# Reordering GpSimd and vector work around two RMS statistics of a Trainium2 step

## The chip, the cores and the metric

The kernel runs on one NeuronCore of a Trainium2 chip. Five engines run side by side, each through its own queue in order: TensorE (PE, with its weight loads PEld), VectorE (DVE), ScalarE (ACT), GpSimd (POOL) and SyncE (SP), which here only issues DMAs. They wait for one another through semaphores. The metric is the device time of one execution in microseconds (us), median over several runs.

## The reference

Two trunk layers over 512 latent tokens and 128 context tokens (640 columns in the kernel) with 1024 features, all in float32. Layer 0 is neighbourhood attention, layer 1 a gated linear recurrence; each is followed by a SwiGLU feed-forward. Every sub-layer is normalised first and added back through a gate, and the result is normalised once more. What matters here is the end of layer 1:

```python
def _rms_norm(x, g):
    return x * lax.rsqrt(jnp.mean(x * x, axis=-1, keepdims=True) + RMS_EPS) * g

def _modulate(x, g, shift, scale):
    return _rms_norm(x, g) * (1 + scale[:, None, :]) + shift[:, None, :]

def _swiglu(x, w_gu, w_down):
    gate, up = jnp.split(x @ w_gu, 2, axis=-1)
    return (jax.nn.silu(gate) * up) @ w_down
...
    o, h = _lru_mixer(...)                       # ends in y @ w_out
    x = x + g1 * o
    x = x + g2 * _swiglu(_modulate(x, norm_g, sh2, sc2), w_gu, w_down)
return _rms_norm(x, final_g)
```

## The kernel before

Features lie on partitions (8 tiles of 128, index k or f), tokens along the free axis. Every float32 matrix product is done as three passes in a reduced format: each operand is split into `hi` (ACT casts it) and `lo` (DVE subtracts `hi` from the original), and PE adds hi·hi, hi·lo and lo·hi in PSUM. So each weight tile costs a DMA into a `raw` buffer (three of them in rotation), an ACT cast into `whi` or `whx` and a DVE subtraction into `wlo` or `wlx`. A raw buffer can be loaded again only when its readers are done.

The order on each engine is set by the program's scheduler: it runs over the code with its own time estimates, and the order in which it issues becomes the queue's order. `self.tc.issue_after(ins)` keeps what is written under it from being issued before `ins`; it sets an order and is no wait by itself.

**The output projection of layer 1** (`project_halves`) works on two halves of 320 tokens, CH[0] and CH[1]. For each output tile f a product (`chunk`) lands in PSUM (tiles `mm`, `mx`), DVE adds it to `x` (`residual`, L424), ACT squares the sum (`sq`, two buffers) and DVE adds the squares up in `ssq` (L373, `square`). The instruction of the last such addition is `self.sq`; the last square goes to PE directly.

**The statistic** (`stat`) then runs across the engines: PE multiplies `ssq` and the last square with a column of ones (`at`, L382 and L385), DVE scales it (`var`, L387), GpSimd raises it to the power -1/2 (`rs`, L389), DVE spreads the result on a diagonal (`dg`, L391), and PE multiplies ones with it, so that each partition has the factors of all tokens (`rr`, L394, in a tile named `mx`). In the projection ACT copies that to SBUF (`r`, L744).

**The second feed-forward** (`ffn_halves`) begins with three plain units (PLAIN = 3): gate and up weights, six weight tiles from `unit`, whose splits stand at L177 and L178. `plain(us, 0)` multiplies them with the first half of the tokens, which was normalised earlier, while the statistic of the second half runs. The first weight tile's product may go ahead of `at`; `held` places the first matmul of the second tile behind `at` and its sixth input tile (k = 5) and all later tiles behind `rr`. Then the second half is normalised (L692, L693), split (`xt` and `big`, L1025, L1026), and `plain(us, 1)` uses it. The other hidden units are done by a Strassen-like scheme over halves: it needs sums of input quarters (`sums`: L712 to L714 on DVE and the last on GpSimd, L715, into x) and of weight quarters (`sum_weights`: four subtractions or additions of 128x512 on GpSimd, tile `sum`, L764, that read the raw gate and up weights of a unit).

**The tail** (`project_last`) does the last part of the down projection in two token chunks, CHL = 384 and 256 tokens. After each chunk comes `stat`; the last tile's product (f = 7) of the second chunk is issued behind `rr` of the first. At the end DVE scales the 16 tiles of x with the factors and the final gain (L467) and SP writes `y`.

Of the kernel before, what the change touches and what calls it, by code (L numbers as in the profile page):

```python
# [9 lines left out]
F32 = mybir.dt.float32  # L10
F32R = mybir.dt.float32r
AF = mybir.ActivationFunctionType
ALU = mybir.AluOpType
AX = mybir.AxisListType

P = 128
# [12 lines left out]
NF = FF // P  # L29
# [14 lines left out]
PLAIN = 3  # L44
# [81 lines left out]
class _Step:  # L126
# [33 lines left out]
        return self.t([P, KT, NTOK + 2], dt, "big", 4)[:, :, 0:n]  # L160


    def unit(self, src, slot=None):
        nc = self.nc
        _, a, b = src.shape
        raw = self.t([P, a, b], F32, "raw", 3)
        nc.sync.dma_start(raw, src)
        if slot is None:
            self.nu += 1
            slot = "x" if self.wx and self.nu % 2 == 0 else "m"  # L170
        if slot == "x":
            hi = self.t([P, a, b], F32R, "whx", 3, self.sb)
            lo = self.t([P, a, b], F32R, "wlx", 3, self.sb)
        else:
            hi = self.t([P, a, b], F32R, "whi", 3)
            lo = self.t([P, a, b], F32R, "wlo", 3)
        nc.scalar.copy(hi, raw)  # L177
        nc.vector.tensor_tensor(lo, raw, hi.bitcast(F32), ALU.subtract)  # L178
        return hi, lo

    def two(self, src, x):
# [192 lines left out]
        self.lastq[t0] = q  # L374

    def stat(self, t0, t1):
        nc = self.nc
        bl = [min(b, t1 - P) for b in range(t0, t1, P)]
        n = len(bl)
        ps = self.ps()  # L380
        for j, b in enumerate(bl):
            nc.tensor.matmul(ps[:, j:j + 1], self.ssq[:, b:b + P], self.ones[:, 0:1], start=True, stop=not self.lastq)  # L382
            if not self.lastq:
                continue
            self.at = nc.tensor.matmul(ps[:, j:j + 1], self.lastq[t0][:, b - t0:b - t0 + P], self.ones[:, 0:1], start=False, stop=True).ins  # L385
        v = self.t([P, 8], F32, "var", 2)[:, 0:n]
        self.var = nc.vector.tensor_scalar(v, ps[:, 0:n], 1.0 / D, EPS, ALU.mult, ALU.add).ins  # L387
        r = self.t([P, 8], F32, "rs", 2)[:, 0:n]
        nc.gpsimd.tensor_tensor(r, v, self.mhalf.broadcast_to([P, n]), ALU.pow)  # L389
        dg = self.t([P, 4, P], F32, "dg", 1, self.sb)[:, 0:n]  # L390
        self.dg = nc.vector.tensor_tensor(dg, self.ident.unsqueeze(1).broadcast_to([P, n, P]), r.unsqueeze(2).broadcast_to([P, n, P]), ALU.mult).ins  # L391
        ps = self.ps("rr" if "rr" in self.ptags else "mx")
        for j, b in enumerate(bl):
            self.rr = nc.tensor.matmul(ps[:, b - t0:b - t0 + P], self.ones, dg[:, j], start=True, stop=True).ins  # L394
        self.r = ps, t0
# [55 lines left out]
    def project_last(self, w, hi, lo, gk):  # L451
        G = self.need(self.gcols, gk)
        us, rs, dst = [], [], self.o["y"].rearrange("(k p) t -> p k t", p=P)
        for f in range(0, KT, 2):
            us += self.two(w[f:f + 2], f % 4)
        for c, (t0, t1) in enumerate(CHL):
            for f, u in enumerate(us):
                with self.tc.issue_after(self.rr) if c and f == KT - 1 else nullcontext():
                    ps = self.chunk(u, hi, lo, t0, t1)
                self.residual(f, t0, t1, ps, G, True)  # L460
            self.stat(t0, t1)
            rs.append(self.r[0])
        for (t0, t1), r in zip(CHL, rs):
            for k in range(KT):
                xs = self.x[:, k, t0:t1]
                with self.tc.issue_after(self.sq if k < 3 else self.var if k < 4 else self.dg) if t0 == 0 else nullcontext():
                    self.nc.vector.scalar_tensor_tensor(xs, xs, self.col("fg", k), r[:, 0:t1 - t0], ALU.mult, ALU.mult)  # L467
                if k % 2:
                    self.nc.sync.dma_start(dst[:, k - 1:k + 1, t0:t1], self.x[:, k - 1:k + 1, t0:t1])
# [238 lines left out]
    def sums(self, k, xd):  # L708
        nc = self.nc
        b11, b12, b21, b22 = [self.x[:, j, a:a + HT] for j in (k, k + KH) for a in (0, HT)]  # L710
        t2 = self.t([P, HT], F32, "c22", 2, self.sb)
        nc.vector.tensor_tensor(b11, b12, b11, ALU.subtract)  # L712
        nc.vector.tensor_tensor(t2, b22, b11, ALU.subtract)
        nc.vector.tensor_tensor(b12, b22, b12, ALU.subtract)  # L714
        nc.gpsimd.tensor_tensor(b21, b21, t2, ALU.subtract)  # L715
        for n, v in (("T1", b11), ("T2", t2), ("T3", b12)):
            self.halve(n, k, v)
        nc.sync.dma_start(self.x[:, k], xd[k * P:k * P + P])
# [37 lines left out]
    def sum_weights(self, q):  # L756
        nc, W, g = self.nc, q["W"], q["g"]
        q["u"], src = self.t([P, KT, P], F32, "raw", 3), q["u"]
        nc.sync.dma_start(q["u"], src)
        ss = [self.t([P, KT, P], F32, "sum", 2, self.sb) for _ in range(2)]  # L760
        s1, s2, s3, s4 = [s[:, a:a + KH] for s in ss for a in (0, KH)]
        g1, g2, u1, u2 = [t[:, a:a + KH] for t in (g, q["u"]) for a in (0, KH)]
        for o, x, y, op in ((s1, u1, u2, ALU.add), (s2, s1, g1, ALU.subtract), (s3, g1, u1, ALU.subtract), (s4, g2, s2, ALU.subtract)):
            nc.gpsimd.tensor_tensor(o, x, y, op)  # L764
        for s, names in zip(ss, (("S1", "S2"), ("S3", "S4"))):
            hi, lo = [self.t([P, KT, P], F32R, n, 3, self.sb) for n in ("whx", "wlx")]
            self.split(hi, lo, s)
            for n, a in zip(names, (0, KH)):
                W[n] = hi[:, a:a + KH], lo[:, a:a + KH]
# [83 lines left out]
                self.sums(j, xd)  # L853

    def ffn_halves(self, l, key, xd):
        us = [[self.unit(self.i["gu"][l, c * NF + f]) for c in range(2)] for f in range(PLAIN)]
        self.hold = True
        self.plain(us, 0)
        self.hold = False
# [12 lines left out]
        for ci, n in enumerate(CHN):  # L872
            for j in range(n):
                f = f0 + j
# [302 lines left out]
```

## Time and profile before

| | |
|---|---|
| median of 3 runs | 1556.68 us (1553.93 to 1560.59) |
| profiled execution | 1557.26 us, span from first to last instruction 1555.5 us |
| busy in the span: PE, PEld, DVE, ACT, POOL | 1490.3, 1444.0, 1067.1, 714.9, 205.8 us |
| mean granted TensorE clock | 0.983 of full speed |
| stretch 1050 to 1100 us | PE busy 48.58 us, DVE 30.20, ACT 22.98, POOL 2.31, clock 0.99 |
| stretch 1100 to 1150 us | PE busy 46.38 us, DVE 34.35, ACT 25.05, POOL 10.74, clock 0.90 |
| stretch 1500 to 1556 us | PE busy 42.80 us, DVE 30.48, ACT 12.42, POOL 1.55, clock 0.86 |

Times in the trace count from the span's start. A row of the timeline reads: start, length, engine, line, operation, output<-input, shapes, number of instructions; in brackets how long the engine was idle before it and whose result ended that. A matmul of 128x320 is shown with 0.31 us, but they overlap: the next one starts about 0.15 us later at full clock. The projection's second half and its statistic lie between about 1080 and 1107 us, the tail from about 1517 us to the end.

### The profile page before, as it was taken

How to read it: one execution, taken by the hardware profiler on the slowest of the kernel's cores; microseconds unless marked ns; L12 is line 12 of the kernel's file. 1: busy time of each engine (PE TensorE's matmuls, PEld its weight loads, DVE VectorE, ACT ScalarE, POOL GpSimd, SP SyncE). 2: the span in 40 equal slices, each digit the busy share in tenths (PEclk: the TensorE clock that was granted, in tenths of full speed). 3: DMA queues.
4: the chain of work that ended last, by engine and by line, in shares of the span. 5: the costliest groups of instructions: out<-in, count | busy, mean ns of one | idle time of the engine just before them, and what ended most of it. 6: DMA issues, size and time to landing. Idle time of an engine off the chain costs nothing. (4 is left out here: it accounts for less than half of the span.)

```text
span 1555.5 us, 26069 instructions
## 1 busy us (share of the span) xinstructions
PE 1490.3 (96%) x10315; PEld 1444.0 (93%) x10315; DVE 1067.1 (69%) x2034; ACT 714.9 (46%) x1321; POOL 205.8 (13%) x231
## 2 busy tenths in 40 slices
PE   5999999989999999999999999969899999999996
PEld 4899899879999999999999888869899999999996
DVE  5678788959999887434446489875755656565646
ACT  4576666655332123212334499763544342424232
POOL 2211122100111110000000000000212323232310
PEclk8999999999999999999999999989899999999997
DMA  9535655535666663222223212124232231313111
GB/s 376 159 114 164 170 168 172 155 116 185 190 190 190 201 197 124 72 83 76 68 84 105 70 62 68 55 96 153 89 124 69 82 109 56 108 55 109 55 55 68
DMA packets 69754, 188.25 MB, mean 121 GB/s; under 512 B 7793, under 2 KB 23297, under 8 KB 69505
## 3 DMA queue, kind: packets, MB, share of 16 engines
q1 hardware_dynamic: 57824, 144.49, 29.5%
q0 software_dynamic: 11520, 41.95, 8.8%
q8 instruction: 81, 1.33, 0.4%
q14 instruction: 41, 0.33, 0.1%
q10 hardware_dynamic: 288, 0.16, 0.0%
HBM read 171.09 MB, written 8.92 MB: 116 GB/s over the span
## 5 line engine op out<-in xcount | busy, mean ns | idle before, releaser
L209 PE MATMUL mm<-big,whi 128*128 128x320 f32 (+2 forms) x1290 | 401.8, 315 | 15.9 <-ACT big L1025 8.9
L210 PE MATMUL mm<-big,whi 128*128 128x320 f32 (+2 forms) x1290 | 404.2, 314 | 1.7 <-DVE big L1026 1.3
L211 PE MATMUL mm<-big,wlo 128*128 128x320 f32 (+2 forms) x1290 | 402.8, 313 | 1.0 <-DVE wlo L178 1.0
L209 PEld LDWEIGHTS mm<-big,whi 128*128 128x128 f32 x1290 | 244.7, 191 | 20.4 <-ACT big L1025 9.8
L210 PEld LDWEIGHTS mm<-big,whi 128*128 128x128 f32 x1290 | 245.6, 190 | 5.1 <-DVE big L1026 3.5
L211 PEld LDWEIGHTS mm<-big,wlo 128*128 128x128 f32 x1290 | 245.1, 190 | 2.5 <-DVE wlo L178 1.4
L239 DVE SCALAR_TENSOR_TENSOR mprod<-mraw,csb 128x1024 f32<-128x1024 f32 x160 | 195.4, 1221 | 14.3 <-DMA mraw<-in_wm 13.6
L177 ACT CAST whi<-raw 128x1024 fp32r<-128x1024 f32 (+1 forms) x90 | 93.3, 1037 | 113.5 <-PE mm L210 80.4
L424 DVE SCALAR_TENSOR_TENSOR x<-mm,G,x 128x128 f32<-128x128 f32 (+3 forms) x211 | 85.2, 434 | 86.7 <-PE mm L211 85.8
L178 DVE TENSOR_TENSOR wlo<-raw,whi 128x1024 fp32r<-128x1024 f32 (+1 forms) x90 | 109.6, 1218 | 29.5 <-ACT whi L177 26.6
L211 PE MATMUL mm<-big,wlx 128*128 128x320 f32 (+3 forms) x363 | 112.6, 310 | 0.0
L210 PE MATMUL mm<-big,whx 128*128 128x320 f32 (+3 forms) x363 | 112.4, 310 | 0.0
L209 PE MATMUL mm<-big,whx 128*128 128x320 f32 (+3 forms) x363 | 112.3, 309 | 0.0
L235 POOL DMA_DIRECT2D mraw<-in_wm x80 | 43.4, 542 | 387.1 <-DVE mprod L239 274.7
L209 PE MATMUL mx<-big,whi 128*128 128x320 f32 (+2 forms) x278 | 86.9, 312 | 0.9 <-DVE big L639 0.9
L210 PE MATMUL mx<-big,whi 128*128 128x320 f32 (+2 forms) x278 | 86.4, 311 | 0.0
L211 PE MATMUL mx<-big,wlo 128*128 128x320 f32 (+2 forms) x278 | 86.3, 311 | 0.0
L389 POOL TENSOR_TENSOR rs<-var,mhalf 128x3 f32<-128x3 f32 (+3 forms) x10 | 9.2, 927 | 556.4 <-DVE var L387 556.4
L177 ACT CAST whx<-raw 128x1024 fp32r<-128x1024 f32 (+1 forms) x40 | 41.0, 1028 | 88.8 <-PE mm L210 53.9
L211 PE MATMUL mx<-big,wlx 128*128 128x320 f32 (+3 forms) x245 | 76.3, 312 | 0.7 <-DVE wlx L178 0.7
L209 PE MATMUL mx<-big,whx 128*128 128x320 f32 (+3 forms) x245 | 76.1, 311 | 0.0
L210 PE MATMUL mx<-big,whx 128*128 128x320 f32 (+3 forms) x245 | 76.0, 310 | 0.0
(291 smaller groups left out, 3609.3 us busy)
## 6 DMA issues: line engine op xcount, KB each, us to landing
raw<-in_gu SPq DMA_DIRECT2D x88, 512.0 KB, 3.5
mraw<-in_wm POOLq DMA_DIRECT2D x80, 512.0 KB, 3.9
raw<-in_dn SPq DMA_DIRECT2D x24, 512.0 KB, 3.6
raw<-in_wqk SPq DMA_DIRECT2D x16, 512.0 KB, 4.8
raw<-in_wi SPq DMA_DIRECT2D x16, 512.0 KB, 3.5
raw<-in_dn SPq DMA_DIRECT2D x16, 448.0 KB, 3.3
sw<-in_wm SPq DMA_DIRECT2D x10, 512.0 KB, 10.2
raw<-in_wv SPq DMA_DIRECT2D x8, 512.0 KB, 3.8
```

Of the source, the lines that this page charges most:

```text
L177: nc.scalar.copy(hi, raw)
L178: nc.vector.tensor_tensor(lo, raw, hi.bitcast(F32), ALU.subtract)
L209: nc.tensor.matmul(ps, hi[:, k], xhi[:, k, s], start=(k == 0), stop=False)
L210: nc.tensor.matmul(ps, hi[:, k], xlo[:, k, s], start=False, stop=False)
L211: nc.tensor.matmul(ps, lo[:, k], xhi[:, k, s], start=False, stop=(k == nk - 1))
L235: nc.gpsimd.dma_start(w, self.i["wm"][l * 6 + j - 2, f])
L239: nc.vector.scalar_tensor_tensor(prod, w, 1.0, self.csb[:, s], ALU.mult, ALU.mult, accum_out=out[:, s, f:f + 1])
L389: nc.gpsimd.tensor_tensor(r, v, self.mhalf.broadcast_to([P, n]), ALU.pow)
L424: self.nc.vector.scalar_tensor_tensor(xs, ps[:, a - t0:b - t0], G[:, s, f:f + 1], xs, ALU.mult, ALU.add)
```

## The change

Four edits, in the words of the code:

- `unit` gets an argument `after`: the split's subtraction on DVE is issued behind that instruction. The four weight tiles of the second and third plain unit (`f` = 1, 2) get the last addition of squares in the projection, `self.sq`; the first unit's two tiles get none.
- `stat` is cut into `moment` (`at`, `var`, `rs`, `dg`) and `spread` (`rr`). Elsewhere they still follow each other.
- `sum_weights` issues its four GpSimd instructions behind `self.pw`, which is the latest power (`rs`), and after `sums(0)` and `sums(1)` the GpSimd subtraction of those (`t4`).
- In the tail the first chunk's `spread` is called inside the second chunk's loop ahead of tile f = 5, where before it stood ahead of the whole second chunk; and of the eight scalings of the first chunk, the first three may go after the first chunk's `dg`, the next three after the last addition of squares.

```diff
-    def unit(self, src, slot=None):
+    def unit(self, src, slot=None, after=None):
...
         nc.scalar.copy(hi, raw)
-        nc.vector.tensor_tensor(lo, raw, hi.bitcast(F32), ALU.subtract)
+        with self.tc.issue_after(after) if after else nullcontext():
+            nc.vector.tensor_tensor(lo, raw, hi.bitcast(F32), ALU.subtract)
...
     def stat(self, t0, t1):
+        self.spread(self.moment(t0, t1))
+
+    def moment(self, t0, t1):
...
-        nc.gpsimd.tensor_tensor(r, v, self.mhalf.broadcast_to([P, n]), ALU.pow)
+        self.pw = nc.gpsimd.tensor_tensor(r, v, self.mhalf.broadcast_to([P, n]), ALU.pow).ins
...
+        return t0, bl, dg
+
+    def spread(self, moment):
+        nc = self.nc
+        t0, bl, dg = moment
         ps = self.ps("rr" if "rr" in self.ptags else "mx")
...
+        first = None
         for c, (t0, t1) in enumerate(CHL):
             for f, u in enumerate(us):
+                if c and f == 5:
+                    self.spread(first)
+                    rs.append(self.r[0])
                 with self.tc.issue_after(self.rr) if c and f == KT - 1 else nullcontext():
                     ps = self.chunk(u, hi, lo, t0, t1)
                 self.residual(f, t0, t1, ps, G, True)
-            self.stat(t0, t1)
-            rs.append(self.r[0])
+            if c:
+                self.stat(t0, t1)
+                rs.append(self.r[0])
+            else:
+                first, dg = self.moment(t0, t1), self.dg
...
-                with self.tc.issue_after(self.sq if k < 3 else self.var if k < 4 else self.dg) if t0 == 0 else nullcontext():
+                with self.tc.issue_after(dg if k < 3 else self.sq if k < 6 else self.var if k < 7 else self.dg) if t0 == 0 else nullcontext():
...
-        nc.gpsimd.tensor_tensor(b21, b21, t2, ALU.subtract)
+        t4 = nc.gpsimd.tensor_tensor(b21, b21, t2, ALU.subtract).ins
+        self.pw = t4 if k < 2 else self.pw
...
-            nc.gpsimd.tensor_tensor(o, x, y, op)
+            with self.tc.issue_after(self.pw):
+                nc.gpsimd.tensor_tensor(o, x, y, op)
...
-        us = [[self.unit(self.i["gu"][l, c * NF + f]) for c in range(2)] for f in range(PLAIN)]
+        us = [[self.unit(self.i["gu"][l, c * NF + f], None, self.sq if f else None) for c in range(2)] for f in range(PLAIN)]
```

The instructions are the same in number and shape on every engine; only their order differs, and only in these stretches. Line numbers of the changed program are higher by up to 18. The rows below are the engines' queues; a number behind a name tells one buffer or tile from another of the same name.

GpSimd before, from the projection's first statistic on (`rs_11500` is the power of the second half's statistic, `x` the subtractions of `sums`):

```order
L389 TENSOR_TENSOR rs_11265<-var_11263,mhalf_68 128x3
L764 TENSOR_TENSOR sum_12009<-raw_12007 128x512
L764 TENSOR_TENSOR sum_12010<-raw_11970,raw_12007 128x512
L764 TENSOR_TENSOR sum_12009<-sum_12009,raw_11970 128x512
L389 TENSOR_TENSOR rs_11500<-var_11498,mhalf_68 128x3
L764 TENSOR_TENSOR sum_12010<-raw_11970,sum_12009 128x512
L715 TENSOR_TENSOR x_10897<-x_10897,c_1882_11815 128x320
L715 TENSOR_TENSOR x_10897<-x_10897,c_1886_11882 128x320
```

and after:

```order
L393 TENSOR_TENSOR rs_11265<-var_11263,mhalf_68 128x3
L393 TENSOR_TENSOR rs_11500<-var_11498,mhalf_68 128x3
L731 TENSOR_TENSOR x_10897<-x_10897,c_1882_11815 128x320
L731 TENSOR_TENSOR x_10897<-x_10897,c_1886_11882 128x320
L782 TENSOR_TENSOR sum_12009<-raw_12007 128x512
L782 TENSOR_TENSOR sum_12010<-raw_11970,raw_12007 128x512
L782 TENSOR_TENSOR sum_12009<-sum_12009,raw_11970 128x512
L782 TENSOR_TENSOR sum_12010<-raw_11970,sum_12009 128x512
```

The four sums of the first Strassen unit have gone from around the power to behind the first two subtractions of `sums`.

DVE before, at the end of the projection (`ssq` is the addition of squares, the last of them `sq_11449`; the splits of the plain units' third to sixth weight tile are `wlo_11526`, which stands further up, `wlx_11532`, also further up, `wlo_11538` and `wlx_11544`; `wul` is a split for the first Strassen unit):

```order
L424 SCALAR_TENSOR_TENSOR x_10897<-mx_11461,G_1341_7628,x_10897 128x128
L178 TENSOR_TENSOR wlo_11538<-raw_11535,whi_11537 128x1024
L1026 TENSOR_TENSOR big_10892<-x_10897,big_10892 128x320
L373 TENSOR_TENSOR ssq_10941<-ssq_10941,sq_11371 128x320
L178 TENSOR_TENSOR wlx_11544<-raw_11541,whx_11543 128x1024
L373 TENSOR_TENSOR ssq_10941<-ssq_10941,sq_11410 128x320
L373 TENSOR_TENSOR ssq_10941<-ssq_10941,sq_11449 128x320
L1026 TENSOR_TENSOR wul_12024<-raw_12007,wuh_12023 128x512
L387 TENSOR_SCALAR var_11498<-at_11491 128x3
L391 TENSOR_TENSOR dg_11502<-ident_63,rs_11500 128x384
L692 SCALAR_TENSOR_TENSOR x_10897<-x_10897,A_1176_6453,r_11255 128x192
```

and after:

```order
L1044 TENSOR_TENSOR big_10892<-x_10897,big_10892 128x320
L374 TENSOR_TENSOR ssq_10941<-ssq_10941,sq_11371 128x320
L374 TENSOR_TENSOR ssq_10941<-ssq_10941,sq_11410 128x320
L374 TENSOR_TENSOR ssq_10941<-ssq_10941,sq_11449 128x320
L179 TENSOR_TENSOR wlo_11526<-raw_11523,whi_11525 128x1024
L179 TENSOR_TENSOR wlx_11532<-raw_11529,whx_11531 128x1024
L179 TENSOR_TENSOR wlo_11538<-raw_11535,whi_11537 128x1024
L391 TENSOR_SCALAR var_11498<-at_11491 128x3
L395 TENSOR_TENSOR dg_11502<-ident_63,rs_11500 128x384
L179 TENSOR_TENSOR wlx_11544<-raw_11541,whx_11543 128x1024
L708 SCALAR_TENSOR_TENSOR x_10897<-x_10897,A_1176_6453,r_11255 128x192
```

Four splits of 128x1024 have moved behind the last addition of squares, three of them ahead of `var` and one behind `dg`; `wul` now stands some 20 rows further on, among the second half's work.

PE before, in the tail, between the first chunk's `at` and the second chunk's next product (`mx_15867` is `rr` of the first chunk):

```order
L385 MATMUL at_15854<-ones_72,sq_15852 128x1
L210 MATMUL mm_15977<-big_11510,whx_15716 128x256
L211 MATMUL mm_15977<-big_11509,wlx_15717 128x256
L209 MATMUL mm_15977<-big_11509,whx_15716 128x256
L210 MATMUL mm_15977<-big_11510,whx_15716 128x256
L211 MATMUL mm_15977<-big_11509,wlx_15717 128x256
L394 MATMUL mx_15867<-dg_15865,ones_72 128x128 x3
L209 MATMUL mx_15871<-big_11509,whi_15698 128x256
```

and after, around `rr` (now `mx_15955`):

```order
L210 MATMUL mm_15977<-big_11509,whx_15716 128x256
L211 MATMUL mm_15977<-big_11510,whx_15716 128x256
L212 MATMUL mm_15977<-big_11509,wlx_15717 128x256
L403 MATMUL mx_15955<-dg_15865,ones_72 128x128 x3
L210 MATMUL mx_15959<-big_11509,whi_15710 128x256
L211 MATMUL mx_15959<-big_11510,whi_15710 128x256
L212 MATMUL mx_15959<-big_11509,wlo_15711 128x256
```

Between the last `at` and `rr` PE has 32 matmuls of 128x256 after the change and 5 before; 24 matmuls are left behind `rr`, where 48 were.

## The prediction

> **What bounds the kernel now.** I read the busy shares first, then short windows around the places that the change touches, then the queues of PE, DVE and GpSimd there.
>
> ```profile
> PE 1490.3 (96%) x10315; PEld 1444.0 (93%) x10315; DVE 1067.1 (69%) x2034; ACT 714.9 (46%) x1321; POOL 205.8 (13%) x231
> 1098.00:1107.00 9.00, 5.38 (x27) 5.01 (x27) 3.33 (x3) 0.62 (x1) 6.25 (x5) 0.58 0.20 64
> 1107.00:1128.00 21.00, 21.00 (x136) 21.00 (x136) 19.86 (x51) 13.85 (x40) 5.04 (x3) 0.93 0.12 37
> ```
>
> PE is busy for 96% of the span, so time is to be had only where PE idles or runs slowly. A window's row gives stretch, length, the busy time of PE, PEld, DVE, ACT and POOL, and then the clock: 0.58 of full speed in the nine microseconds around the second half's statistic. Between 1107 and 1128 us PE has no hole; there it has none until the tail either, so what is won ahead of it goes through to the end, unless something that feeds PE is late.
>
> The projection's second statistic, on PE, DVE and POOL:
>
> ```profile
> 1095.08 0.31 PE L845 MATMUL mm<-big,wlo 128*128 128x320 f32 x1
> 1096.71 0.38 PE L382 MATMUL at<-ones,ssq 128*128 128x1 f32 x2 [1.32 <-DVE ssq L373]
> 1105.35 1.62 PE L394 MATMUL mx<-dg,ones 128*128 128x128 f32 x6 [3.62 <-DVE dg L391]
> 1106.62 0.61 PE L843 MATMUL mm<-big,whx 128*128 128x320 f32 x1
> 1109.87 0.31 PE L843 MATMUL mx<-big,whi 128*128 128x320 f32 x1
> ...
> 1091.91 0.67 DVE L424 SCALAR_TENSOR_TENSOR x<-mx,G,x 128x192 f32<-128x192 f32 x2
> 1092.51 1.21 DVE L178 TENSOR_TENSOR wlo<-raw,whi 128x1024 fp32r<-128x1024 f32 x1
> 1093.64 0.48 DVE L1026 TENSOR_TENSOR big<-x,big 128x320 fp32r<-128x320 f32 x1
> 1094.04 0.48 DVE L373 TENSOR_TENSOR ssq<-ssq,sq 128x320 f32<-128x320 f32 x1
> 1098.74 1.64 DVE L1026 TENSOR_TENSOR wul<-raw,wuh 128x512 fp32r<-128x512 f32 x1 [2.08 <-ACT wuh L1025]
> 1100.30 0.15 DVE L387 TENSOR_SCALAR var<-at 128x3 f32<-128x3 f32 x1
> 1103.59 1.62 DVE L391 TENSOR_TENSOR dg<-ident,rs 128x384 f32<-128x384 f32 x1 [3.14 <-POOL rs L389]
> ...
> 1101.49 1.25 POOL L764 TENSOR_TENSOR sum<-sum,raw 128x512 f32<-128x512 f32 x1
> 1102.71 0.85 POOL L389 TENSOR_TENSOR rs<-var,mhalf 128x3 f32<-128x3 f32 x1
> 1103.54 1.25 POOL L764 TENSOR_TENSOR sum<-raw,sum 128x512 f32<-128x512 f32 x1
> ```
>
> PE waits twice, 1.32 us for the additions of squares and 3.62 us for `dg`. The additions end late because splits of about 1.13 us (start 1092.51 to 1093.64) stand between them. `var` (1100.30) waited behind `wul`; the power was ready to start at about 1100.45 and began at 1102.71, behind sums; `dg` took 1.62 us beside the fourth sum. The projection's first statistic shows the same chain with none of this beside it:
>
> ```profile
> 1072.63 0.28 PE L385 MATMUL at<-ones,sq 128*128 128x1 f32 x2
> 1074.47 0.15 DVE L387 TENSOR_SCALAR var<-at 128x3 f32<-128x3 f32 x1
> 1075.65 0.56 DVE L391 TENSOR_TENSOR dg<-ident,rs 128x384 f32<-128x384 f32 x1 [1.03 <-POOL rs L389]
> 1079.21 0.83 PE L394 MATMUL mx<-dg,ones 128*128 128x128 f32 x6
> 1079.80 0.39 PE L209 MATMUL mx<-big,whi 128*128 128x320 f32 x1
> ```
>
> From the start of `var` to the end of `dg` it takes 1.74 us there (1074.47 to 1076.21) and 4.91 us (1100.30 to 1105.21) here; from the start of `at` to that of `var` 1.84 us.
>
> **The change part by part.** *Splits behind the additions.* The last residual (1091.91) comes with PE's product and does not move. Behind it DVE has 0.60 for that residual, 0.40 for the split of `big` and three additions of the same shape, 0.40 each (1093.64 to 1094.04 for one), which ends at 1094.1; with 0.3 for squares that wait for their buffers, 1094.4. So `at` no longer waits: it follows the first plain tile at 1095.24, 1.47 us earlier, and is done by 1097.1 (1.84 us later) at the latest. But three splits now stand ahead of `var`: 1094.4 + 3 x 1.13 = 1097.8, so `var` starts at 1097.9, set by DVE and not by `at`. That is 2.4 us earlier than before.
>
> *Sums behind the power.* The power finds POOL idle and `dg` runs alone: 1.74 us from 1097.9, plus the 0.14 us between `dg` and `rr` (1105.21 to 1105.35), so `rr` starts at 1099.8 instead of 1105.35: 5.55 us. PE still idles there, since the 15 matmuls between `at` and `rr` take 2.2 us at 0.15 each: with some 1.1 us for `at` itself (my estimate, inside those 1.84) they are over at 1098.5, and a gap of 1.3 us is left in place of 3.62.
>
> What is left open is the clock. Before, it had fallen to half, so that `rr` took 1.27 us (1105.35 to 1106.62) where the first statistic's took 0.59. The nearest row of a short gap shortly after an `at` is in the tail (1533.28, below): 1.17 us, and half clock behind it. So I take 5.6 us with no gain from the clock. The other end is full clock throughout: 0.68 us in `rr`, and the twelve matmuls behind it took 3.25 us (1106.62 to 1109.87), where twelve at 0.15 take 1.8; 1.4 more, together 2.1, so 7.7 us. The Trainium skill, "TensorE: Matmul & The Clock Gate", Part 1, says that the clock is halved after an idle window of about 3.4 us, so by it a gap of 1.3 us would leave it full and the middle would gain 7.7 us. The tail's row does not agree with that: half clock after 1.17 us.
>
> *What the moved work could hold up.* The third plain unit's second raw weight tile can be loaded only after the third tile's split:
>
> ```profile
> 1093.74 0.33 SPq L759 DMA_DIRECT2D raw<-in_gu  x1
> 1098.09 0.62 ACT L1025 CAST wuh<-raw 128x512 fp32r<-128x512 f32 x1 [0.95 <-DMA raw<-in_gu]
> 1107.47 0.68 DVE L692 SCALAR_TENSOR_TENSOR x<-x,A,r 128x192 f32<-128x192 f32 x2 [2.26 <-ACT r L744]
> 1121.22 0.48 DVE L1026 TENSOR_TENSOR xt<-x,xt 128x320 fp32r<-128x320 f32 x1
> 1125.86 0.31 PE L844 MATMUL mm<-xt,whi 128*128 128x320 f32 x1
> sw<-in_wm SPq DMA_DIRECT2D x10, 512.0 KB, 10.2
> ```
>
> Such a load took 4.35 us from issue to the cast (1093.74 to 1098.09). The plain tile's is now issued at 1095.6 and lands at 1099.95; its cast on ACT ends at 1101.0, beside `rr`, and ahead of the copy `r` (which ended before 1107.47). Its split ends on DVE at about 1102.2, and then the second half is normalised, 5.2 us earlier than 1107.47. `wuh`, which stands on ACT behind `r` and ahead of the normalisations, is issued at 1097.9 and lands at 1102.3: at most 0.3 us. The other loads on SP stand behind these in the same order as before.
>
> *Four sums beside DVE's work.* They now run at some 1113 to 1120 us, in the stretch where DVE is busy 19.86 of 21 us, mostly with operations on two SBUF inputs. What one sum costs DVE: `wul` took 1.64 us beside sums, against a mean of 0.69 us later; `dg` 1.62 against 0.56.
>
> ```profile
> L1026 DVE TENSOR_TENSOR wul<-raw,wuh 128x512 fp32r<-128x512 f32 x18 | 12.4, 690 | 0.8 <-ACT wuh L1025 0.4
> ```
>
> About 1 us for each sum; if only half of a sum meets a DVE operation, half of that: 2 to 4.2 us for four. `wul`, 0.69 us, has moved into that stretch too. The tightest user I found is the fourth `xt` split: ready at 1121.7, used by PE at 1125.86, 4.2 us of slack. After the change PE is there 5.55 us earlier and DVE 5.2 - 0.7 = 4.5 us earlier, slack 3.1 us; two or three of the four sums come ahead of that split, so 1 to 3 us. I take no cost; the bounds are 0 and 1.1 us (4.2 - 3.1), and with full clock, where PE comes 2.1 us earlier still, 1.0 to 3.2 us. A rule of the Trainium skill speaks against this step: "GPSIMD Engine Reference", section "Key points", says that GpSimd shares its SBUF interfaces with VectorE and contends with DVE instructions that have two SBUF inputs. The trace agrees (1.64 against 0.69 us), and by the rule taken to its end, every sum in full, the cost would be the upper bound.
>
> *The tail.*
>
> ```profile
> 1533.28 1.65 PE L394 MATMUL mx<-dg,ones 128*128 128x128 f32 x6 [1.17 <-DVE dg L391]
> 1534.58 0.56 PE L209 MATMUL mx<-big,whi 128*128 128x256 f32 x1
> 1536.54 0.29 PE L209 MATMUL mx<-big,whi 128*128 128x256 f32 x1
> 1541.04 0.28 PE L211 MATMUL mx<-big,wlo 128*128 128x256 f32 x1
> 1543.51 0.58 PE L382 MATMUL at<-ones,ssq 128*128 128x1 f32 x2 [2.20 <-DVE ssq L373]
> 1546.95 1.20 PE L394 MATMUL mx<-dg,ones 128*128 128x128 f32 x4 [1.57 <-DVE dg L391]
> ...
> 1541.35 0.61 DVE L424 SCALAR_TENSOR_TENSOR x<-mx,G,x 128x128 f32<-128x128 f32 x2
> 1542.50 0.95 DVE L373 TENSOR_TENSOR ssq<-ssq,sq 128x256 f32<-128x256 f32 x2 [0.54 <-ACT sq L371]
> 1543.37 1.66 DVE L467 SCALAR_TENSOR_TENSOR x<-x,cols,mx 128x384 f32<-128x384 f32 x3
> 1546.72 5.32 DVE L467 SCALAR_TENSOR_TENSOR x<-x,cols,mx 128x384 f32<-128x384 f32 x12
> ```
>
> 27 more matmuls ahead of `rr`, at 0.118 us (1536.54 to 1541.04, 38 steps) 3.2 us of work, cover the gap of 1.17. With the gap the half clock goes: `rr` 0.59 (as in the first statistic) instead of 1.30 (1533.28 to 1534.58), and the nine matmuls behind it 1.07 instead of 1.96 (1534.58 to 1536.54). PE's stream ends 1.17 + 0.71 + 0.89 = 2.8 us earlier. Behind it `at` waited 2.20 us; now two products lie behind `rr` instead of four, the earlier squares are done, and what is left is a residual and two additions, 0.61 + 0.95 = 1.6: 0.6 us more. Three of the first chunk's scalings now run while PE still multiplies, 3 x 0.55 = 1.7 us of DVE work that PE's 24 matmuls hide. Then the end: of the last twelve scalings four (2.2 us) are the first chunk's, and they run 3.9 us beyond the end of `rr` (1548.15 to 1552.04). Afterwards only the second chunk's eight lie behind `rr`, 5.32 - 2.2 = 3.1 us: 0.8 us. Together 4.2 us; 3.4 if the squares gain nothing and the residuals are pushed behind the scalings by 0.2, and 5.0 if the last `at`, shown here at half clock, runs at full.
>
> **The sum.** 5.6 + 4.2 = 9.8 us. The profiled execution took 1557.26 us (span 1555.5), so 1547.5; the median of the runs, 1556.68, lies 0.58 below it, which gives 1546.9 us.
>
> **The rivals.** *Full clock in the middle*: speaks for it that PE's weak stretch shrinks from 9 us to about 4; against it the tail's row. 2.1 us more, and less DVE's lateness of 0 to 1: about 1544. *Contention*: DVE, slowed by the sums, delivers `xt` or the following splits late and PE waits about 3 us; for it the 1.64 of `wul`, against it the 3.1 us of slack. 1550. The profile would show PE idle at the first matmuls on `xt`. *A part does not do what it says*: the middle's chain stays as long, since the additions still end late behind ACT's squares or `var` behind later splits, and half of the 5.6 us stays: with the tail about 1550 to 1552; or the tail alone: 1552.5. *Slower*: the load for `wuh` lands late, and on ACT its cast holds up all normalisations of the second half. From the first normalisation (1107.47) to the end of the fourth `xt` split (1121.70) took 14.2 us, and with `wul` between them it will take 14.9; that split has to be ready at 1120.3 for no loss, so the loss begins with a landing near 1105, 7 us after the issue. To eat the 9.8 us as well it must land some 17 us after it. The longest median of a load of this size is 10.2 us (`sw`), so this would cost 3 us, not the sign.
>
> **How the numbers follow.** Forecast 0.48 (1546.9, own range 1545 to 1549), full clock 0.20 (1544), contention 0.20 (1550), half a change 0.08 (1552), slower 0.04. Half a per cent, about what a measurement tells from no change here, is 7.8 us, so faster begins below 1548.9: three quarters and more of the forecast, all of the full clock, a fifth of the contention, 0.62 in all. Within 0.5% the rest, 0.34; slower 0.04. The range reaches from full clock with the tail's best end, 1542.3, to the tail alone, 1552.
>
> **What would show it.** Right: `at` follows PE's plain tile without idle time; three splits of 1.13 us, `var`, the power within 0.4 us of it, `dg` of 0.56 us; PE idle about 1.3 us before `rr`, not 3.62; the sums behind the subtractions into x; no PE gap where `xt` is used first; in the tail `rr` without idle time, at full clock. Wrong: more than 2 us of idle PE before the second `rr`; PE gaps between it and the tail, or DVE's splits of 320 columns at 0.9 us and more beside the sums with PE waiting for them; a tail that ends less than 3 us after the old distance from its last `at`.

## The result, and the profile after

The changed kernel took 1547.09 us in the median of 6 runs (1544.95 to 1551.24), the kernel before 1556.65 (6 runs); the ratio is 0.9941 (95% interval 0.9922 to 0.9959). The profiled execution took 1548.14 us, its span is 1546.4 us. 1546.9 us was forecast. By the two profiled executions the gain is 9.1 us, where the sum gave 9.8. That the sum comes out is in good part luck: two terms of it were off, by 2.0 us one way and by 3.7 the other, and a third by 0.6.

The statistic of the projection's second half, from PE's timeline of the changed kernel (start, length, line, operation; in brackets the idle time and what ended it):

```profile
1094.71 0.31 PE L863 MATMUL mm<-big,wlo 128*128 128x320 f32 x1
1094.86 0.28 PE L386 MATMUL at<-ones,ssq 128*128 128x1 f32 x2
1099.42 0.91 PE L403 MATMUL mx<-dg,ones 128*128 128x128 f32 x6 [0.86 <-DVE dg L395]
1100.08 0.40 PE L861 MATMUL mm<-big,whx 128*128 128x320 f32 x1
1101.93 0.31 PE L861 MATMUL mx<-big,whi 128*128 128x320 f32 x1
1120.49 0.42 PE L862 MATMUL mm<-xt,whi 128*128 128x320 f32 x1 [1.83 <-DVE xt L1044]
```

`at` has no idle time ahead of it, `rr` waits 0.86 us instead of 3.62, and the twelve matmuls behind it take 1.85 us (1100.08 to 1101.93) where they took 3.25: full clock. New is the last row: PE stands idle for 1.83 us until the fourth `xt` split is there. The windows behind that wait, with the granted clock as the third number from the end:

```profile
1121.00:1122.00 1.00, 1.00 (x9) 1.00 (x8) 1.00 (x4) 0.00 (x0) 0.00 (x0) 0.97 0.00 0
1122.00:1123.00 1.00, 1.00 (x6) 1.00 (x5) 1.00 (x4) 0.00 (x0) 0.00 (x0) 0.50 0.00 0
1123.00:1124.00 1.00, 1.00 (x5) 1.00 (x5) 1.00 (x4) 0.00 (x0) 0.00 (x0) 0.50 0.88 284
1124.00:1125.00 1.00, 1.00 (x5) 1.00 (x5) 1.00 (x4) 0.51 (x2) 0.00 (x0) 0.50 0.48 87
1125.00:1126.00 1.00, 1.00 (x8) 1.00 (x7) 1.00 (x4) 1.00 (x2) 0.61 (x1) 0.83 0.79 277
```

One and a half microseconds after the wait's end the clock falls to half, for 3.4 us (a window's 0.97, 0.50 three times and 0.83, with half clock as 0.50). What made `xt` late, from the timelines of DVE and GpSimd:

```profile
1097.53 0.15 DVE L391 TENSOR_SCALAR var<-at 128x3 f32<-128x3 f32 x1
1098.71 0.56 DVE L395 TENSOR_TENSOR dg<-ident,rs 128x384 f32<-128x384 f32 x1 [1.03 <-POOL rs L393]
1101.20 3.37 DVE L708 SCALAR_TENSOR_TENSOR x<-x,A,r 128x192 f32<-128x192 f32 x11
1112.46 5.69 DVE L1044 TENSOR_TENSOR big<-x,big 128x320 fp32r<-128x320 f32 x4
1118.07 1.56 DVE L730 TENSOR_TENSOR x<-x 128x320 f32<-128x320 f32 x1
1119.55 0.48 DVE L1044 TENSOR_TENSOR big<-x,big 128x320 fp32r<-128x320 f32 x1
1119.96 0.48 DVE L1044 TENSOR_TENSOR xt<-x,xt 128x320 fp32r<-128x320 f32 x1
...
1097.83 0.85 POOL L393 TENSOR_TENSOR rs<-var,mhalf 128x3 f32<-128x3 f32 x1 [22.59 <-DVE var L391]
1113.24 1.55 POOL L782 TENSOR_TENSOR sum<-raw 128x512 f32<-128x512 f32 x1
...
1117.88 1.40 POOL L782 TENSOR_TENSOR sum<-raw,sum 128x512 f32<-128x512 f32 x1
```

The power comes at once behind `var` and `dg` takes 0.56 us, as forecast. But beside the four sums (the first and the last are shown) five operations of DVE last from 1112.46 to 1119.55, 7.1 us, for work of 0.40 us each.

The tail, on PE:

```profile
1530.54 0.83 PE L403 MATMUL mx<-dg,ones 128*128 128x128 f32 x6
1531.12 0.36 PE L210 MATMUL mx<-big,whi 128*128 128x256 f32 x1
1533.94 0.28 PE L212 MATMUL mm<-big,wlx 128*128 128x256 f32 x1
1535.87 0.35 PE L386 MATMUL at<-ones,ssq 128*128 128x1 f32 x2 [1.65 <-DVE ssq L374]
1538.76 1.20 PE L403 MATMUL mx<-dg,ones 128*128 128x128 f32 x4 [1.86 <-DVE dg L395]
```

`rr` has no idle time and takes 0.58 us. To compare kernels without what drifts earlier in an execution, I use two stretches of each profile. The middle reaches from the first half's `rr` to the first product of the first Strassen unit; the rest from there to the end of the span. What drifts is large: the first half's `rr` starts between 1076.3 and 1081.1 us in the thirteen profiles, ahead of the stretch that the change reorders, so a microsecond or two between the medians of two of them says little. Before, these two instructions start at 1079.21 and 1144.63 us, after, at 1078.84 and 1140.34:

```profile
1144.63 0.31 PE L786 MATMUL mx<-big,whi 128*128 128x320 f32 x1
```

```profile
1078.84 0.83 PE L403 MATMUL mx<-dg,ones 128*128 128x128 f32 x6
1140.34 0.31 PE L804 MATMUL mx<-big,whi 128*128 128x320 f32 x1
```

So the middle took 65.42 and takes 61.50, a gain of 3.9 us; the rest took 410.87 (1555.5 - 1144.63) and takes 406.06 (1546.4 - 1140.34), a gain of 4.8. The missing 0.4 us of the 9.1 is that drift.

| kernel | ratio to before (95%) | middle, us | rest, us |
|---|---|---|---|
| before | 1 | 65.42 | 410.9 |
| changed | 0.9941 (0.9922 to 0.9959) | 61.50 | 406.1 |
| tail only | 0.9964 (0.9950 to 0.9978) | 65.34 | 406.1 |
| middle only | 0.9970 (0.9958 to 0.9981) | 61.41 | 409.3 |
| splits only | 0.9954 (0.9940 to 0.9968) | 59.38 | 410.5 |
| sums only | 0.9979 (0.9965 to 0.9993) | 61.70 | 410.8 |
| changed, sums untied | 0.9929 (0.9917 to 0.9942) | 59.76 | 405.3 |
| changed, sums on DVE | 0.9928 (0.9914 to 0.9942) | 57.85 | 405.8 |
| changed, sums behind the third subtraction | 0.9919 (0.9905 to 0.9934) | 57.84 | 406.0 |
| changed, sums in halves | 0.9926 (0.9913 to 0.9938) | 59.87 | 405.5 |
| sums behind the third, two splits ahead of `var` | 0.9917 (0.9901 to 0.9933) | 56.76 | 406.4 |

The intervals of the last five overlap with one another and with the changed kernel's; what tells those kernels apart is the middle of their profiles, one execution each. The rest goes from 405.3 to 406.4 us among the kernels with the new tail and from 409.3 to 410.9 among those with the old one; the 409.3 of the middle alone is taken up below.

### The profile page after: what moved, and what is told of

The parts are those of the page before. It is cut to its first block, busy times and chain, and to the rows that moved or that the text cites. A ratio compares the mean times of both kernels' runs of the same rounds, so it can differ in the third digit from the quotient of the medians.

```text
span 1546.4 us, 26062 instructions
## 1 busy us (share of the span) xinstructions
PE 1487.3 (96%) x10315; PEld 1441.6 (93%) x10315; DVE 1071.4 (69%) x2034; ACT 714.2 (46%) x1321; POOL 210.4 (14%) x231
## 4 chain that ended last, share of the span: by engine, by line
PE 82%; DVE 7%; ACT 6%; issue 2%; DMA 2%; SPq 0%; POOL 0%; POOLq 0%; DVEq 0%; ACTq 0%
PE mm L211 13%; PE mm L212 13%; PE mm L210 13%; PE mx L210 5%; PE mx L212 5%; PE mx L211 5%; PE mx L804 3%; PE mx L805 3%; PE mx L806 3%; PE op L646 2%; PE tp L570 1%; PE mc L804 1%; PE mc L806 1%; PE mc L805 1%; PE mm L226 1%
```

## The experiments

In the diffs a minus is the changed kernel and a plus the experiment. Gains in microseconds behind a ratio are worked out from that ratio; the medians of the first four runs give 1.2 to 1.6 us less each (4.4, 3.4, 5.9 and 1.6).

**Each part alone.** The tail alone leaves the middle as it was:

```diff
-            with self.tc.issue_after(self.pw):
+            with nullcontext():
                 nc.gpsimd.tensor_tensor(o, x, y, op)
...
-        us = [[self.unit(self.i["gu"][l, c * NF + f], None, self.sq if f else None) ...
+        us = [[self.unit(self.i["gu"][l, c * NF + f], None, None) ...
```

> Only the tail's edits; splits and sums stand as in the kernel before. If the two places are independent, the tail alone gives what the changed kernel's trace shows from its first at of the tail on, about 5 us: 1551.6 us. By the prediction's own sum it gives 4.2: 1552.5. If the tail's gain needed the earlier work (for example that PE reaches it at another phase of the clock), it gives 3 us or less: 1553.7 or more. In the trace: no idle time before the tail's first rr, 0.6 us for rr instead of 1.3, at about 1.7 us behind PE's last product instead of 2.2.

Measured: 1551.08 us, ratio 0.9964, 5.6 us; the profile's rest 406.1, 4.7 us less than before, as in the changed kernel, and the middle 65.34. In these profiles the two places do not touch each other.

The middle alone: the tail's loop and scalings as in the kernel before.

> Splits and sums as in the changed kernel, the tail as before. Contention theory: rr 5.6 us earlier and another 2.0 from the full clock, then 1.8 us of waiting for the fourth xt split and some 1.6 us of half clock behind that: 4 us in all, 1552.6 us. By the prediction as written (half clock, no wait) 5.6 us: 1551. The two are close in time, so the trace decides: PE idle at the first product on xt, or not.

Measured: 1552.09 us, ratio 0.9970, 4.7 us. The middle is 61.41 us, as in the changed kernel, and the wait is there again, with half clock behind it:

```profile
1121.36 0.42 PE L855 MATMUL mm<-xt,whi 128*128 128x320 f32 x1 [1.75 <-DVE xt L1037]
```

Then the middle in its two parts. The splits alone (the sums without their order, the tail as before):

> Of the middle only the four splits move behind the last addition; GpSimd's sums get no order of their own, the tail is as before. Since the raw tiles of the sums now load later, they stand behind the power anyway, but directly behind it, ahead of the subtractions into x. So at, var, power and dg come as in the changed kernel, and the sums run at about 1102.5 to 1108 us, beside the normalisations instead of beside the splits of big. Contention theory: DVE loses about as much there (4 to 5 us), PE waits for the fourth xt split by 1 to 3 us, time as with both parts, 1552.6 us. Rival (only the splits of 320 columns suffer, or DVE is late for another reason such as wul and the later load): with the sums gone from that place the wait is gone or unchanged at 1.83 us whatever the sums do, and DVE's operations beside them keep their length; time 1549 or 1552.6.

Measured: 1549.57 us, ratio 0.9954, 7.2 us. The intervals of this kernel and of the middle alone overlap, but the middle is 2 us shorter, 59.38 against 61.41. That is 3 us under the time expected by the contention and near its rival's 1549, so the time alone would have spoken for the rival; the profile decides. The path is the same (0.86 us ahead of `rr`), and the sums now stand directly behind the power. Rows of DVE and GpSimd in this kernel:

```profile
1098.65 3.38 DVE L701 SCALAR_TENSOR_TENSOR x<-x,A,r 128x192 f32<-128x192 f32 x11
1102.34 5.38 DVE L701 SCALAR_TENSOR_TENSOR x<-x,A,r 128x128 f32<-128x128 f32 x5
1113.76 2.37 DVE L1037 TENSOR_TENSOR big<-x,big 128x320 fp32r<-128x320 f32 x4
1100.51 2.69 POOL L775 TENSOR_TENSOR sum<-raw 128x512 f32<-128x512 f32 x1 [4.36 <-DMA raw<-in_gu]
```

The loss has moved with the sums: five normalisations take 5.38 us, where they take 1.53 in the changed kernel, and the four splits of `big` are back from 5.69 to 2.37. The rival that only the splits suffer is out. Part of the sums' time cost DVE less here, since the first sum was the one that was slowed (2.69 us), not the eleven normalisations beside it (3.38 us, 3.37 in the changed kernel). PE's wait at `xt` is 1.27 us instead of 1.83, and no half clock follows it. So the order given to the sums was not needed for the power (the later loads put them behind it anyway) and cost 2.0 us of the middle (61.41 against 59.38): 0.5 of wait and the half clock behind it.

The sums alone (the splits and the tail as before):

> Of the middle only the sums move behind the power and the first two subtractions into x; splits and tail are as before. at still waits 1.3 us for the additions. var stands behind wul, but wul is now alone (0.69 instead of 1.64 us), so var starts near 1099.4, and 1.74 us later dg is done: rr near 1101.3, 4 us earlier than before. The clock: it had fallen at 1099.5 before any wait for dg, so I expect half clock at rr again (1.27 us). The sums make DVE late by 4 to 5 us as in the changed kernel, PE waits 0 to 1 us at xt. 3 us faster in all: 1553.7 us. Rival: if the sums cost DVE nothing, 4 us: 1552.7; if the sums' place was not what held the power, no gain.

Measured: 1553.83 us, ratio 0.9979, 3.3 us. `wul` took 0.69 us, `var` started at 1099.73, `rr` took 1.13 us at half clock:

```profile
1097.35 0.38 PE L386 MATMUL at<-ones,ssq 128*128 128x1 f32 x2 [1.32 <-DVE ssq L374]
1102.03 1.48 PE L403 MATMUL mx<-dg,ones 128*128 128x128 f32 x6
1122.67 0.41 PE L855 MATMUL mm<-xt,whi 128*128 128x320 f32 x1 [1.27 <-DVE xt L1037]
```

Either part alone gets about as much of the middle as both, or more: 3.7 and 6.0 us, together 4.0. The wait at `xt` is over the 0 to 1 us that were expected: PE comes there 1.7 us later than in the changed kernel (41.55 us behind the first half's `rr` against 39.82), but DVE is later too.

**The wait at `xt`.** The changed kernel with the sums untied (the first line of the diff above alone):

> The changed kernel without the order of the sums: they stand directly behind the power, ahead of the two subtractions into x. With the splits alone PE waited 1.27 us at xt instead of 1.83 and the clock stayed full behind that wait; so this should end 1.5 to 2.5 us before the changed kernel: 1545 us, about 11 us below the kernel before. Rival: what the splits alone gained over both parts was no effect of the sums' place, and this equals the changed kernel, 1547.

Measured: 1545.96 us; the middle is 59.76, 1.7 us less than in the changed kernel. The wait is 1.64 us, not 1.27, since here DVE gave way to all four sums (the eleven normalisations took 7.54 us), but the clock stays full behind it.

With the four sums on DVE, GpSimd idle there (`self.lo` is the latest split of an activation, `self.first` holds for the first Strassen unit only):

```diff
+            self.b22 = self.lo
...
-            with self.tc.issue_after(self.pw):
-                nc.gpsimd.tensor_tensor(o, x, y, op)
+            with self.tc.issue_after(self.b22 if self.first else self.pw):
+                (nc.vector if self.first else nc.gpsimd).tensor_tensor(o, x, y, op)
+        self.first = False
```

> The changed kernel, but the first Strassen unit's four sums are done by DVE, behind the last B22 split, and GpSimd does none of them there. Contention theory: the splits of 320 columns beside the old place take 0.40 us again from start to start, the fourth xt split is ready some 5 us earlier, the wait of 1.83 us at xt and the half clock behind it are gone, and DVE pays 4 x 0.61 us later where it has slack: 3.4 us faster than the changed kernel, 1543.7 us. Rival (DVE is late at xt because of wul and the later load, not because of GpSimd): PE still waits 1 us or more at xt; 1546 to 1547.

Measured: 1546.43 us, where 1543.7 was expected: in time not told apart from the changed kernel, and what the rival had said. But the middle is 57.85 us, 3.65 less, without any wait at `xt`; the profiled execution was 2.25 us behind the changed kernel's at the first half's `rr` already. Its DVE:

```profile
1114.68 2.37 DVE L1046 TENSOR_TENSOR big<-x,big 128x320 fp32r<-128x320 f32 x4
1117.38 0.48 DVE L1046 TENSOR_TENSOR big<-x,big 128x320 fp32r<-128x320 f32 x1
1118.98 0.68 DVE L783 TENSOR_TENSOR sum<-raw 128x512 f32<-128x512 f32 x1
```

From the first of the four splits to the one behind the subtraction it is 2.70 us, against 7.09 in the changed kernel: the four sums on GpSimd cost DVE 4.4 us, 1.1 each, where DVE itself does one in 0.61. `wul` and the later loads are the same in both, so the lateness was the sums'.

The sums left on GpSimd, but behind the third subtraction:

```diff
-        self.pw = t4 if k < 2 else self.pw
+        self.pw = t4 if k < 3 else self.pw
```

> The changed kernel, but the sums stay behind the third subtraction into x too (some 127 us past 1000 instead of 113), where DVE has gaps. Contention theory: no wait at xt, 3 us faster than the changed kernel, 1544 us, unless the load that waits for the sums' raw tiles (down weights) now comes late: then PE waits near 1140 us and part is lost. Operations of DVE beside the sums take 1.2 to 1.6 us there too.

Measured: 1544.25 us, ratio 0.9919; the middle is 57.84 us, as expected, without a wait at `xt` or near 1140. DVE beside the sums, in this kernel (`g` reads PSUM, the others two SBUF tiles):

```profile
1121.16 1.57 DVE L1044 TENSOR_TENSOR big<-x,big 128x320 fp32r<-128x320 f32 x1
1122.65 0.48 DVE L823 TENSOR_TENSOR g<-mm,g 128x320 f32<-128x320 f32 x1
1123.05 2.27 DVE L1044 TENSOR_TENSOR big<-c,big 128x320 fp32r<-128x320 f32 x2
...
1122.34 1.55 POOL L782 TENSOR_TENSOR sum<-raw,raw 128x512 f32<-128x512 f32 x1
```

The loss is the same, and costs nothing, because there nobody waits for these splits. The operation with an input from PSUM kept its 0.48 us beside the second sum.

The sums in two instructions each, at the changed kernel's place:

```diff
-            with self.tc.issue_after(self.pw):
-                nc.gpsimd.tensor_tensor(o, x, y, op)
+            for c in (0, 2) if self.first else (0,):
+                e = c + 2 if self.first else KH
+                with self.tc.issue_after(self.pw):
+                    nc.gpsimd.tensor_tensor(o[:, c:e], x[:, c:e], y[:, c:e], op)
+        self.first = False
```

> The changed kernel, but each of the four sums of the first Strassen unit is two instructions of 256 columns at the same place. If one DVE operation gets through for each GpSimd instruction (in the changed kernel four DVE splits and one subtraction took about 1.5 us each beside four sums of about 1.5 us), eight instructions let eight DVE operations through, at 0.7 to 0.8 us each: DVE loses about 2.5 to 3 us instead of 5.4, no wait or under 0.3 us at xt, 1544 us. Rival (what counts is the time or the bytes that GpSimd moves): DVE loses the same 5 us, the wait stays near 1.8 us, 1547 us.

Measured: 1545.7 us, middle 59.87:

```profile
1111.27 1.94 POOL L784 TENSOR_TENSOR sum<-raw 128x256 f32<-128x256 f32 x2
...
1114.43 1.02 DVE L730 TENSOR_TENSOR x<-x 128x320 f32<-128x320 f32 x1
1116.32 1.01 DVE L1047 TENSOR_TENSOR xt<-x,xt 128x320 fp32r<-128x320 f32 x1
```

One operation of DVE gets through for each GpSimd instruction, as expected, but half a sum takes 0.96 us and not half of 1.55, and the DVE operations beside it as long. Until the end of the fourth `xt` split DVE loses 3.4 us instead of 4.4, where 2.5 to 3 had been expected (from `rr`'s start it takes 19.9 us, in the changed kernel 21.0, with the sums on DVE 16.6). PE waits 0.8 us at `xt` and 0.6 us for a `g` behind it: shorter, but not gone as expected, and at full clock.

**The clock behind a wait.** Two kernels lengthen the gap ahead of the middle's `rr` by moving matmuls from before it to behind it; both have the sums behind the third subtraction, where the gap is 0.86 us, the clock full and the middle 57.84. The first kernel's edit (the second has 1 in place of the 3):

```diff
-        if not self.hold or not n or k not in (0, 5):
+        if not self.hold or not n or k not in (0, 3):
```

> The changed kernel with the sums behind the third subtraction, and only nine matmuls instead of fifteen between at and rr in the projection's second half: the gap ahead of rr grows from 0.86 to about 1.7 us, everything else stays. If the clock of PE falls with the length of that gap (the reason of the prediction's lower end, where 1.17 us in the tail had gone with half clock), rr takes 1.3 us and the matmuls behind it run 0.27 us apart for 3 us: 0.9 us of gap made up by 0.9 us less work before it, plus 2.1 us of half clock; the stretch from the first rr to the first product of the next unit takes 60.8 us instead of 57.84. If a gap of that length is not enough, the stretch takes 58.7.

> As before, with three matmuls between at and rr: a gap of about 2.6 us. Both views expect half clock here: 59.6 us for the stretch by the gap alone, and 2.1 us more, 61.7, with half clock behind it. If even here the clock stays full, it hangs on something else than idle time between at and rr.

Measured in one execution each: middle 58.74 and 61.14 us. A gap of 1.74 us cost only the 0.9 of the moved work; one of 2.62 cost 3.3, of which 1.5 are half clock. From the two kernels' timelines and windows (the first kernel's, then the second's):

```profile
1100.31 0.91 PE L403 MATMUL mx<-dg,ones 128*128 128x128 f32 x6 [1.74 <-DVE dg L395]
1102.31:1103.31 1.00, 1.00 (x9) 1.00 (x8) 1.00 (x5) 0.05 (x1) 0.00 (x0) 1.00 0.24 36
```

```profile
1100.68 0.91 PE L403 MATMUL mx<-dg,ones 128*128 128x128 f32 x6 [2.62 <-DVE dg L395]
1101.68:1102.68 1.00, 1.00 (x6) 1.00 (x5) 1.00 (x2) 0.37 (x1) 0.00 (x0) 0.52 0.60 242
1102.68:1103.68 1.00, 1.00 (x6) 1.00 (x5) 1.00 (x5) 0.00 (x0) 0.00 (x0) 0.50 0.35 90
1103.68:1104.68 1.00, 1.00 (x6) 1.00 (x5) 1.00 (x4) 0.49 (x1) 0.00 (x0) 0.50 0.73 200
1104.68:1105.68 1.00, 1.00 (x7) 1.00 (x7) 1.00 (x5) 1.00 (x4) 0.00 (x0) 0.77 0.49 181
```

**The last 0.86 us.** Two splits ahead of `var` instead of three, and the sums behind the third subtraction:

```diff
-        ... None, self.sq if f else None) ...
+        ... None, (None, self.sq, self.dg)[f]) ...
```

> The changed kernel with the sums behind the third subtraction, and with two splits instead of three ahead of var (the third plain unit's first goes behind dg). var starts 1.13 us earlier, at is done just before it, and the gap of 0.86 us ahead of rr closes: PE gains 0.9 us there. But the raw loads for the third unit's second tile and the Strassen unit's stand behind that split and land 1.1 us and 2.5 us later, the normalisations start 1.1 us later, and PE is at the fourth xt split 0.9 us earlier; its slack there is about 1.9 us, so 0 to 0.3 us of waiting. 0.6 to 0.9 us faster than without it: 1543.5 us. If the later loads hold up ACT, PE waits 1 us or more at xt and it is no gain.

Measured: 1542.9 us, ratio 0.9917; the middle is 56.76, 1.1 us less, with no wait at `rr` and none at `xt`. It has the lowest median and the shortest middle of all versions, 13.4 us below the runs of before taken with it (1556.29). That it beats the changed kernel, or the one before it in the table, rests on the middle of the profiles; the ratios' intervals overlap.

## Why the prediction was right in its sum, and where it was wrong

*Splits behind the additions, sums behind the power: right.* `at` follows the plain tile, `var` comes behind three splits, the chain from `var` to `dg` takes 1.74 us (1097.53 to 1099.27). `rr` started 5.93 us earlier, 5.56 once the 0.37 us are taken off by which PE was ahead at the first half's `rr` already; 5.55 was forecast. The gap ahead of it was 0.86 us (1.3 forecast). But the second edit added nothing here: with the splits alone `rr` comes as early.

*The clock: wrong choice between the two ends.* The step took the tail's row, a gap of 1.17 us with half clock behind it, as the nearest, and so no gain from the clock. The clock stayed full, and the stretch without any later wait is 57.84 us, 7.58 less than before; the other end had said 7.7. By the rule of the Trainium skill ("TensorE: Matmul & The Clock Gate", Part 1) that was weighed there, full clock was to be expected; but the same rule, an idle window of about 3.4 us, does not give the half clock behind waits of 1.75, 1.83 and 2.62 us. Neither the row alone nor the rule alone decided it. My own row was a bad neighbour: only five matmuls lay between that `at` and its gap, where the middle had fifteen. And the row is not even the same in every execution. In the profile of the middle alone, whose tail is the old one, the gap is 1.17 us again, but `rr` behind it takes 0.69 us instead of 1.30, at full clock:

```profile
1529.71 0.94 PE L403 MATMUL mx<-dg,ones 128*128 128x128 f32 x6 [1.17 <-DVE dg L395]
1530.40 0.36 PE L210 MATMUL mx<-big,whi 128*128 128x256 f32 x1
```

*Sums beside DVE's work: the term that was set to nothing.* "I take no cost" is the step that failed. Its parts were nearly right: DVE lost 4.4 us to four sums (2 to 4.2 had been bounded, a little less), and the step said that with full clock the wait at `xt` would be 1.0 to 3.2 us; it was 1.83. What failed was its count: all four sums came ahead of the `xt` split, not two or three. And the wait brought a cost that the sum had no term for, half clock behind it, 61.50 - 57.84 - 1.83 = 1.8 us. Half clock of that length behind that wait was met in two of the profiles, this one and that of the middle alone. So the middle gave 3.9 us, not 5.6: 2.0 more from the clock, 3.7 less from contention. As cases, full clock (1544) and contention (1550) were listed as alternatives; they came together, and the first made the second. Without the sums the split is ready 37.2 us behind the first half's `rr` (sums on DVE), and PE comes to it at 39.7, 1.4 us earlier than planned: 2.5 us of slack, where 3.1 had been reckoned. The 4.4 us that DVE lost left 1.9 of them as a wait.

*The tail: right in kind, 0.6 us too low.* 4.8 us against 4.2. (Against the old tail in the middle-only profile, 409.3 us, where the clock had stayed full at `rr`, it would be 3.2.) PE's last product came 2.8 us earlier relative to the first chunk's `at`, as forecast (11.01 us from that `at` before, 8.52 after, and of these 0.35 because `at` now stands three matmuls further ahead). The wait of the last `at` fell by 0.55 us (0.6 forecast) and the end by 0.9 (0.8 forecast). The remaining 0.55 us is the last `at` at full clock, the upper end of the range that the prediction gave.

*Slower by a late load: not seen.* `wuh` was cast at 1102.54, within 0.3 us of the forecast.

*The cases' figures.* Two of them do not follow from the prediction's own terms: full clock is 1546.9 - 2.1 = 1544.8 us, not 1544, and full clock with the tail's best end 1556.7 - 7.7 - 5.0 = 1544.0, not 1542.3.

*When the clock falls.* In these profiles it fell behind waits of 1.75 and 1.83 us at `xt` and not behind 1.27 and 1.64; at `rr` behind 2.62 and not behind 1.74. But in the kernel before, in the sums-only kernel and in the old tail it fell with no single wait over 1.32 us, where `at`, whose matmuls have one column, lay close to the gap. Length alone does not explain these.

A count over the thirteen traces sorts them. All changes of the granted clock in an execution lie whole multiples of 3.41 us apart (in the changed kernel at 1121.94, 1125.35 and 1538.36 us, 1 and 121 steps), a grid of steps that runs on whatever PE does. Add up in each step of full clock PE's idle time and the time of `at`: in the middle and in the tail the clock fell behind every step with 1.75 us or more of them, and behind none with 1.74 or less.

So the old tail's half clock was chance: before, 1.26 us of `at` and 0.87 of the gap lay in one step; with the middle alone, 1.26 and 1.17 lay in two. In the changed middle fifteen matmuls keep `at` (1.25 us) and the gap of 0.86 too far apart for any step to hold 1.75. And the wait of 1.83 us at `xt` brings half clock only where a step holds nearly all of it, by this count (an estimate: (3.41 - 1.83 + 2 x 0.08) / 3.41) in about half of its possible places.

No kernel was built to test this, the two sides of the boundary lie 0.01 us apart, and elsewhere in the program the same count sorts less well (a step with 1.51 us fell, one with 1.91 did not), so what exactly is counted stays open.

## What to carry to other kernels

Price work that is moved to an idle engine by what it does to its neighbours: here four sums of 0.61 us each on VectorE cost VectorE 1.1 us each when GpSimd did them beside it, and they were free only where nobody waited for VectorE's results. When one bottleneck is relieved, compute the next buffer's slack with the *best* outcome of the first step, since a gain that comes out larger than planned is what uses the slack up. And a short wait of TensorE can cost twice: 1.83 us of idle time brought another 1.8 of half clock, in the executions where it did. One profile is not enough to read that off: the old tail's gap of 1.17 us went with half clock in three profiles and with full clock in a fourth.

## What the runs showed of the hardware that was not expected

DVE operations with two SBUF inputs and GpSimd's instructions took turns, mostly one for one: beside sums of 1.55 us each split of 320 columns took about 1.4 us instead of 0.40, beside half sums of 0.96 us about 0.95. So it is the number and length of GpSimd's instructions that sets the loss, and short DVE operations lose most: a split of 128x1024 beside a subtraction took 1.90 us instead of 1.22. Who gives way is not fixed: beside the eleven normalisations of the splits-only kernel it was GpSimd's first sum that took 2.69 us, and DVE lost nothing; with the sums untied the same eleven took 7.54 us instead of 3.37 beside sums of 1.29 to 1.41. Why was not tested.

Half clock, once granted, lasted 3.4 us in two profiles, behind the wait of 1.83 us at `xt` and behind the gap of 2.62 us at `rr` (windows of 0.52, 0.50, 0.50 and 0.77 there), where PE had no further gap; in the middle of the kernel before, where the 3.62 us of idle PE fell into it, 10.2 us. The Trainium skill, "TensorE: Matmul & The Clock Gate", Part 1, gives about 3.4 us of work until the clock is full again; that agrees.
